# Two silu gates moved from the mixer stage into the merge, as pairs of seven products

## The chip, the cores and the metric

The kernel runs on one core of a Trainium2 chip. A core has five engines with an instruction queue each: TensorE (PE in the profile; its weight loads are PEld), VectorE (DVE), ScalarE (ACT), GpSimd (POOL) and SyncE (SP), which here only issues transfers. The metric is the device time of one execution in microseconds, lower is better.

## What is computed

One decoder layer over 1024 positions of width 1024, float32. Cut to what matters here:

```
h = rms_norm(x, norm_g) * (1 + scale) + shift          # shift, scale, gate from c @ w_ada
a_q, a_kv, a_g, a_z, b_q, b_k, b_v, b_z, c_.., d_.. = split(h @ w_in)
y_a = nsa_attention(...)             # compressed, selected and window parts
y_b = banded_attention(..., sink)    # window of 128
y_c = stick_breaking_attention(...)
y_d = retention(...)
for i, (y, z) in enumerate(((y_a, a_z), (y_b, b_z), (y_c, c_z), (y_d, d_z))):
    yi = y * silu(z)                              # 1024 x 256
    term = sigmoid(h @ w_merge[i]) * (yi @ w_br[i])
    merged = term if merged is None else merged + term
out = rms_norm(x + gate * (merged @ w_out), final_g)
```

The change is about `a_z` to `d_z`, above all the gates `silu(z)` of branches D and B.

## The kernel before

**Number format.** Every operand of a large matmul is split into a rounded high part and the rest (`hh` and `hl` for `h`, `whi` and `wlo` for weights, `yh` and `yl` for a branch's result, `phi` and `plo` for `w_br`). A product is three matmuls: high by high, rest by high, high by rest. The high part is a copy on ScalarE, the rest a subtraction on VectorE or GpSimd that follows it.

**Stages.** (1) A prologue loads x and `w_ada` and makes `h` (`hh`, `hl`), stored transposed: 8 blocks of 128 channels by 1024 positions. (2) The mix computes the four attention branches. It consists of groups, named by branch and pair of heads (`C0a`, `C0b`, `D0`, `C1`, `D1`, `A0`, `A1`, `B0`, `B1`), each of some units (front and back), and of items. An item is a projection of `h` onto 128 columns of `w_in`: 8 blocks x 3 matmuls x 2 halves of 512 positions = 48 matmuls of 128x512, a weight load of 512 KB and its split. Items with no dependence on the groups fill TensorE between the groups' short matmuls. (3) The merge takes the branches in the order C, D, A, B and computes `h @ w_merge[i]`, mostly as a Strassen-like scheme: a pair of two 128-channel tiles by two 512-position halves takes 7 products of 12 matmuls (`product`) in place of 8. The stationary sides come from the pair's two weight tiles (`op(n)`), the moving sides are seven fixed arrays `MOVING = [b11, T2, T1, b21, T3, b22, b12]`, four of them quarters of `h`, three sums of these. For 4 tiles (`PLAIN`) the product is plain. Behind each product `term` multiplies `yi @ w_br[i]` (6 matmuls on `yh`, `yl`) with the gate. (4) The w_out block loads w_out (`wr`), makes sums of its quarters (`w_jobs`), and computes the last tiles of the merge beside it. (5) The output block does merged @ w_out in 4 pairs of 7 products, adds x and applies the last norm; 124 us from the end of the merge's pairs to the last matmul.

**Order.** Within a stage the program notes its operations with their dependences first, and a list scheduler (`Program.schedule`, line 320 on) then writes an order for each engine, by a priority: a rank by dependence plus a number from two tables, `SHIFT_PE` and `SHIFT`, keyed by the label of the operation. Each engine runs its operations strictly in the order written. `noted(tc, late)` opens such a block; with `late` over zero the scheduler takes all engines but TensorE and SyncE as taken for the first `late` ns, since they are still at work from the block before. Three blocks are opened so: the merge with 8000, the w_out block and the output block with 0.

**Names.** All noted instructions carry line 380 (`issue`, which calls them) in the profile, so they are told apart by tiles. `s`, `d`, `t`, `y` are PSUM tiles of the pools; `y<-hi,RV` are the attention's last products. In the order rows further down, a tile has its buffer's number behind it.

**The gate items.** `z_item` (line 690) is an item whose result z goes to ScalarE (`tanh` of z/2), VectorE ((tanh + 1) * z) and GpSimd (times y), half by half; for branches A, B and D the product is then written to DRAM (`yd`) from GpSimd's queue. D's and C's items (`it_zcd`) stand after A's query items, A's between B's, and B's (`it_zb`) are held until groups `B0` and `B1`. In the merge `y_load` and `y_part` read `yd` back and split it into `yh` and `yl`; for the first branch, C, the split is made from SBUF ahead of the merge (line 403 in the profile).

**The sums.** `t_unit(k)`, k = 0 to 3 (label `sums`), makes `T2`, `T1`, `T3` and the last quarter's difference from `hh` and `hl`: 12 VectorE operations, 4 copies on ScalarE, 1 subtraction on GpSimd and 8 writes to DRAM (`td`) for each k. It stands after the item `it_zcd[1]`.

**Start of the last blocks.** The w_out block begins with the four loads of `wr`. `w_jobs` then splits the first quarter (`tt<-wr` on ScalarE, the subtraction on VectorE), and one of its steps is taken with each step of the plain tiles. The output block begins with the split of the fourth sum of w_out (`wt<-wst`, four on ScalarE and four on VectorE; label `wt4`) and the loads of the gate and of the final norm's scale (`gateb`, `fgb`).

Of the kernel before, what the change touches and what calls it, by code (L numbers as in the profile page):

```python
# [88 lines left out]
def chunks(w):  # L89
# [21 lines left out]
    ('first', 2): 700, ('first', 3): 10000, ('first', 5): -9990, ('first', 6): 10100,  # L111
# [3 lines left out]
    ('item', 10): -97, ('item', 11): 10033, ('item', 12): 9910, ('item', 17): 9997,  # L115
    ('item', 18): 10000, ('item', 19): 21000, ('item', 2): -9903, ('item', 20): 0,
# [77 lines left out]
class Program:  # L194
# [128 lines left out]
    def schedule(self):  # L323
# [11 lines left out]
        for i in range(len(ops)):  # L335
            if left[i] == 0:
                heapq.heappush(later[ops[i].eng], (0.0, i))
        order = []
        dma = warm = 0.0
        port = {"pool": 0.0, "dve": 0.0}  # L340
        turned = False
        while len(order) < len(ops):
# [1718 lines left out]
```

## Time and profile before

| | us |
|---|---|
| median of 3 runs | 1078.72 (1078.55 to 1079.52) |
| the profiled execution | 1079.71 |
| its span | 1077.9 |
| TensorE busy in the span | 1040.4 |
| VectorE busy | 796.5 |
| ScalarE busy | 584.4 |
| GpSimd busy | 435.5 |

The mean granted clock of TensorE over the profiled execution is 0.988 of full speed. The profile is read by stage, since the shares differ by stage: the mix from 21.5 to 587.2 us, the merge from there to 944.2 us, and the last two blocks to 1068.5 us. In the timeline the start of a matmul is recorded and its end modelled, so the distance of two starts tells more than a duration.

### The profile page before, as it was taken

How to read it: one execution, taken by the hardware profiler on the slowest of the kernel's cores; microseconds unless marked ns; L12 is line 12 of the kernel's file. 1: busy time of each engine (PE TensorE's matmuls, PEld its weight loads, DVE VectorE, ACT ScalarE, POOL GpSimd, SP SyncE). 2: the span in 40 equal slices, each digit the busy share in tenths (PEclk: the TensorE clock that was granted, in tenths of full speed). 3: DMA queues.
4: the chain of work that ended last, by engine and by line, in shares of the span. 5: the costliest groups of instructions: out<-in, count | busy, mean ns of one | idle time of the engine just before them, and what ended most of it. 6: DMA issues, size and time to landing. Idle time of an engine off the chain costs nothing.

```text
span 1077.9 us, 16022 instructions
## 1 busy us (share of the span) xinstructions
PE 1040.4 (97%) x5391; PEld 873.4 (81%) x5391; DVE 796.5 (74%) x1797; ACT 584.4 (54%) x1281; POOL 435.5 (40%) x483
## 2 busy tenths in 40 slices
PE   5999999999999999999999999999999999998996
PEld 4778888889878898888888788888888888876885
DVE  5559976986558877999875346777785565489897
ACT  5699964994348866767874232333333233346343
POOL 4623214213525466655464122255454555430002
PEclk8999999999999999999999999999999999999998
DMA  9763311102321113314313913322322232262232
GB/s 338 259 201 80 83 25 48 33 21 59 54 79 40 30 40 101 107 62 134 103 55 124 350 53 88 98 69 69 88 88 58 54 90 73 73 230 74 77 107 95
DMA packets 117606, 105.47 MB, mean 98 GB/s; under 512 B 15260, under 2 KB 96212, under 8 KB 116756
## 3 DMA queue, kind: packets, MB, share of 16 engines
q1 hardware_dynamic: 116048, 99.95, 30.3%
q0 software_dynamic: 1408, 4.48, 1.3%
q8 instruction: 42, 0.69, 0.3%
q14 instruction: 40, 0.33, 0.1%
q10 hardware_dynamic: 68, 0.02, 0.0%
HBM read 81.88 MB, written 17.83 MB: 93 GB/s over the span
## 4 chain that ended last, share of the span: by engine, by line
PE 70%; DVE 11%; ACT 6%; issue 5%; DMA 5%; POOL 2%; SPq 1%; POOLq 0%; ACTq 0%; DVEq 0%
PE d L380 25%; PE s L380 22%; PE t L380 14%; PE y L380 8%; DVE SP L380 4%; ACT t L380 2%; DVE lo L380 1%; DMA wst<-in_w_merge_dram 1%; DVE t L380 1%; ACT SP L380 1%; ACT whi L380 1%; DVE FA L380 1%; POOL RA L380 1%; DMA RA<-RA 1%; ACT hi L380 1%
## 5 line engine op out<-in xcount | busy, mean ns | idle before, releaser
L380 POOL TENSOR_TENSOR wlo<-wst,whi 128x512 fp32r<-128x512 f32 (+1 forms) x108 | 143.3, 1337 | 214.4 <-ACT whi L380 208.8
L380 PE MATMUL d<-hh,whi 128*128 128x512 f32 x440 | 180.5, 410 | 2.5 <-ACT hh L380 1.8
L380 ACT ACTIVATE whi<-wst 128x512 fp32r<-128x512 f32 (+2 forms) x121 | 89.0, 739 | 164.7 <-PE s L380 47.3
L380 PE MATMUL d<-hh,wlo 128*128 128x512 f32 x440 | 173.4, 394 | 0.0
L380 PE MATMUL d<-hl,whi 128*128 128x512 f32 x440 | 173.0, 394 | 0.0
L380 PEld LDWEIGHTS d<-hh,wlo 128*128 128x128 f32 x440 | 83.4, 190 | 18.7
L380 PEld LDWEIGHTS d<-hh,whi 128*128 128x128 f32 x440 | 83.6, 190 | 15.3 <-ACT hh L380 2.0
L380 DVE TENSOR_TENSOR lo<-t,hi 128x512 fp32r<-128x512 f32 (+2 forms) x132 | 79.8, 624 | 18.2 <-ACT hi L380 17.4
L380 PEld LDWEIGHTS d<-hl,whi 128*128 128x128 f32 x440 | 83.5, 190 | 11.6 <-DVE hl L380 0.4
L380 ACT ACTIVATE hi<-t 128x512 fp32r<-128x512 f32 (+3 forms) x148 | 73.8, 525 | 31.4 <-PE t L380 26.9
L380 POOL TENSOR_TENSOR acc<-acc,mt 128x512 f32<-128x512 f32 x44 | 68.0, 1547 | 44.3 <-DVE mt L380 43.7
L380 PE MATMUL s<-hh,whi 128*128 128x512 f32 x200 | 80.4, 402 | 3.9 <-ACT whi L380 3.9
L380 PE MATMUL s<-hh,wlo 128*128 128x512 f32 x200 | 79.7, 398 | 0.9 <-DVE wlo L380 0.9
L380 PE MATMUL s<-hl,whi 128*128 128x512 f32 x200 | 78.5, 394 | 0.0
L380 PE MATMUL t<-kbt,SP 128*128 128x128 f32 (+1 forms) x470 | 68.3, 274 | 6.8 <-DMA kbt<-in_kb_dram 6.4
L380 POOL TENSOR_SCALAR SP<-SP,den,gates 128x640 f32<-128x640 f32 (+7 forms) x64 | 52.9, 835 | 52.9 <-DVE den L380 20.7
L380 ACT ACTIVATE SP<-SP,mx 128x257 f32<-128x257 f32 (+9 forms) x96 | 62.3, 651 | 11.9 <-DVE mx L380 10.7
L380 DVE TENSOR_TENSOR mt<-s,mt 128x512 f32<-128x512 f32 x61 | 41.2, 686 | 36.4 <-PE s L380 36.1
L380 PEld LDWEIGHTS t<-kbt,SP 128*128 128x128 f32 (+1 forms) x470 | 54.7, 141 | 14.2 <-DMA kbt<-in_kb_dram 6.4
L380 PE MATMUL s<-tt,whi 128*128 128x512 f32 x192 | 59.1, 389 | 0.0
L380 ACT ACTIVATE mt<-mt 128x512 f32<-128x512 f32 x56 | 35.1, 629 | 35.4 <-DVE mt L380 35.2
L380 ACT ACTIVATE t<-t 128x512 f32<-128x512 f32 (+5 forms) x97 | 50.1, 522 | 1.1
(343 smaller groups left out, 2717.7 us busy)
## 6 DMA issues: line engine op xcount, KB each, us to landing
wst<-in_w_merge_dram SPq DMA_DIRECT2D x32, 512.0 KB, 4.8
wst<-in_w_in_dram SPq DMA_DIRECT2D x26, 512.0 KB, 3.9
td<-FA SPq DMA_DIRECT2D x32, 256.0 KB, 2.4
tt<-td SPq DMA_DIRECT2D x6, 1024.0 KB, 10.2
FA<-in_x_dram SPq DMA_DIRECT2D x8, 512.0 KB, 5.5
pst<-in_w_br_dram SPq DMA_DIRECT2D x32, 128.0 KB, 2.2
ga<-in_w_ada_dram SPq DMA_DIRECT2D x16, 256.0 KB, 3.1
wr<-in_w_out_dram SPq DMA_DIRECT2D x4, 1024.0 KB, 9.1
```

Source lines behind the costliest of these rows:

```text
L380: fn(*args, **kw)
```

## The change

1. `z_item` is no longer used for D and B. Their weights are loaded as items of the merge (`it_z`), two in front of D's and two in front of B's. The list of pairs gets an entry `(i, -1)` in front of branches 1 (D) and 3 (B): the two 128-column tiles of z by two halves as 7 products. The four quarters that come out are gated by the new `y_part`: tanh on ScalarE, two operations on VectorE, then the split into `yh` and `yl`; `y_load` reads the ungated y back, a quarter at a time, into a buffer shared with `term`. Branch A keeps the old way (renamed `y2_load`, `y2_part`).
2. y of D and B is written to DRAM ungated by SyncE at the end of each of their groups.
3. `t_unit` and the write of `hd` come after group `D1`, where they came after `it_zcd[1]`.
4. `op(7q + 6)` comes one step earlier in a pair.
5. The w_out block is opened with `late` 2000, the output block with 6000; in such a block the scheduler also takes the first transfer as later by `late` + 1100 ns, and TensorE as warm from the start.
6. The `wt4` splits and the loads of `gateb` and `fgb` move from the head of the output block to its second product.
7. Both tables are new throughout; `SHIFT` now has entries for the merge's pairs (`out` and `op` with numbers from 0 on).

```diff
 SHIFT_PE = {
-    ('A0', 0): -9000, ('A0', 1): 19710, ('A0', 11): -10020, ('A0', 14): -10000, ('A0', 15): -10300,
+    ('A0', 1): 1000, ('A0', 10): -9800, ('A0', 11): -10020, ('A0', 12): 9700, ('A0', 13): 0,
...
-        dma = warm = 0.0
+
+        dma, warm = (self.late + 1100.0, 3400.0) if self.late else (0.0, 0.0)
...
-    it_zcd = [z_item(c0 + P * p, br, p) for br, c0 in (("D", D_Z), ("C", C_Z)) for p in range(2)]
+    it_zc, it_za = [[z_item(c0 + P * p, br, p) for p in range(2)] for br, c0 in (("C", C_Z), ("A", A_Z))]
...
-    it_za = [z_item(A_Z + P * p, "A", p) for p in range(2)]
-    it_zb = [z_item(B_Z + P * p, "B", p) for p in range(2)]
...
-    it_zb[0].after = "B0"
-    it_zb[1].after = "B1"
...
+    it_z = []
+    for c0 in (D_Z, B_Z):
+        for p in range(2):
+            it = add_item()
+            mtile_weights(it, [win(c0 + P * p)])
+            it_z.append(it)
     n_mix = len(order)
-    order = order + it_m
+    for i in range(4):
+        order = order + it_z[i - 1:i + 1] * (i % 2) + it_m[8 * i:8 * i + 8]
...
+            if name[0] in "DB":
+                sy.dma_start(yd["DAB".index(name[0]), int(name[1])], Y[name[0], int(name[1])])
             md.bulk = True
+            if name == "D1":
+                for v in range(2):
+                    sy.dma_start(hd[v], b12[v].bitcast(F32))
+                for k in range(4):
+                    md.label = "sums", k
+                    t_unit(k)
...
-            if it is it_zcd[1]:
-                for v in range(2):
-                    sy.dma_start(hd[v], b12[v].bitcast(F32))
-                for k in range(4):
-                    md.label = "sums", k
-                    t_unit(k)
...
-        pairs = [(i, j) for i in range(4) for j in range(4) if (i, 2 * j) not in PLAIN]
+
+        pairs = [(i, j) for i in range(4) for j in range(-(i % 2), 4) if (i, 2 * j) not in PLAIN]
+        real = [q for q, (i, j) in enumerate(pairs) if j >= 0]
...
+        def y_load(q, e, n):
+            sy.dma_start(keep[5 - q % 2], yd[pairs[q][0] - 1, e][:, n * 512:n * 512 + 512])
...
+        def y_part(q, e, n, z, s):
+
+            y = keep[5 - q % 2]
+            se.activation(s, z, AF.Tanh, scale=0.5)
+            ve.scalar_tensor_tensor(z, s, 1.0, z, op0=ALU.add, op1=ALU.mult)
+            ve.tensor_tensor(z, z, y, ALU.mult)
+            ypart(z, e, n)
...
+            if z:
+                y_part(q, 0, 1, t1, ga)
+                y_load(q, 1, 0)
+                y_part(q, 1, 0, u3, u2)
+                return
...
-        with md.noted(tc):
+        with md.noted(tc, 2000.0):
...
-        with md.noted(tc):
-            md.label = "wt4", 0
-            for k in range(4):
-                parts(wt4, k, t4f[k], ve)
-            sy.dma_start(gateb, gd.partition_broadcast(P))
-            sy.dma_start(fgb, final_g.partition_broadcast(P))
+        with md.noted(tc, 6000.0):
...
+                if q == 0:
+                    md.label = "wt4", 0
+                    for k in range(4):
+                        parts(wt4, k, t4f[k], ve)
+                    sy.dma_start(gateb, gd.partition_broadcast(P))
+                    sy.dma_start(fgb, final_g.partition_broadcast(P))
```

How the order written out moves, at three places. A row is one instruction (or some alike) with what it writes and reads.

VectorE at the end of group D1 and the start of A0, before: `yt<-y,mv,rs` is D's last norm, the `RW`, `RA` and `vcr` rows are preparation of branch A.

```order
L380 TENSOR_SCALAR yt_150<-y_137,mv_166,rs_167 128x64
L380 TENSOR_TENSOR t_129<-t_129 32x128
L380 TENSOR_SCALAR yt_150<-y_137,mv_166,rs_167 128x64
L380 COPY sg_168<-t_127 128x32
L380 SCALAR_TENSOR_TENSOR RW<-d_133,kbt,RW 64x512
L380 TENSOR_TENSOR RA<-s_136,RA 64x32 x2
L380 TENSOR_TENSOR vcr<-s_134,vcr 32x64
L380 SCALAR_TENSOR_TENSOR RW<-d_133,kbt,RW 64x512
L380 TENSOR_TENSOR vcr<-s_134,vcr 32x64
L380 TENSOR_TENSOR RA<-d_132,RA 64x512 x2
```
The same place after the change; the `FA` rows are the sums of `t_unit`:

```order
L438 TENSOR_SCALAR yt_150<-y_137,mv_166,rs_167 128x64 x2
L438 TENSOR_TENSOR RW<-t_131,RW 128x512
L438 TENSOR_TENSOR RA<-SP,RA 64x4x64 x4
L438 TENSOR_TENSOR FA<-FA 128x512
L438 TENSOR_TENSOR FA<-FA,hh 128x512
L438 TENSOR_TENSOR FA<-FA,hl 128x512
L438 TENSOR_TENSOR FA<-hh,FA 128x512
L438 SCALAR_TENSOR_TENSOR RW<-d_132,kbt,RW 64x512 x2
L438 TENSOR_TENSOR t_129<-t_129,s_135 32x256
L438 TENSOR_TENSOR FA<-FA 128x512
L438 TENSOR_TENSOR t_129<-t_129 32x128
```
The sums now begin beside the preparation of A; before, the first of them came behind A0's units.

TensorE at the end of the mix, before: `y<-hi,RV` are branch B's last attention products, `d<-hh,whi` and `s<-hh,whi` are bulk matmuls, and 24 of the `s` rows follow before the first `d<-yh,phi`, a matmul on the split result of branch C.

```order
L380 MATMUL y_137<-hi_143,RV 128x256
L380 MATMUL y_137<-lo_149,RV 128x256
L380 MATMUL d_133<-hh,whi_138 128x512
L380 MATMUL d_133<-hl,whi_138 128x512
L380 MATMUL d_133<-hh,wlo_139 128x512
L380 MATMUL d_133<-hh,whi_138 128x512
L380 MATMUL d_133<-hl,whi_138 128x512
L380 MATMUL d_133<-hh,wlo_139 128x512
L380 MATMUL s_134<-hh,whi_141 128x512
L380 MATMUL s_134<-hl,whi_141 128x512
```
After:

```order
L438 MATMUL y_137<-hi_143,RV 128x256
L438 MATMUL y_137<-lo_149,RV 128x256
L438 MATMUL s_134<-hh,wlo_142 128x512
L438 MATMUL s_134<-hh,whi_141 128x512
L438 MATMUL s_134<-hl,whi_141 128x512
L438 MATMUL s_134<-hh,wlo_142 128x512
L438 MATMUL d_133<-yh,phi_5542 128x512
L438 MATMUL d_133<-yl,phi_5542 128x512
L438 MATMUL d_133<-yh,plo_5543 128x512
```
Four bulk matmuls now stand between the last attention product and the first one that reads `yh`.

ScalarE at the head of the output block, before: `whi<-acc` and `whi<-s` are high parts of stationary sides for the products, `wt<-wst` the four copies of the fourth sum of w_out.

```order
L380 ACTIVATE mt_5803<-t_127 128x512
L380 ACTIVATE whi_141<-acc 128x512
L380 ACTIVATE hh<-wr_8148 128x512
L380 ACTIVATE whi_141<-acc 128x512
L380 ACTIVATE wt_8475<-wst_125 128x512 x2
L380 ACTIVATE wt_8475<-wst_126 128x512 x2
L380 ACTIVATE whi_138<-s_5801 128x512
L380 ACTIVATE mt_5802<-t_140 128x512
```
After:

```order
L438 ACTIVATE whi_141<-acc 128x512
L438 ACTIVATE whi_138<-acc 128x512
L438 ACTIVATE hh<-wr_8164 128x512
L438 ACTIVATE mt_5566<-s_134 128x512
L438 ACTIVATE whi_141<-s_5565 128x512
L438 ACTIVATE wt_8487<-wst_125 128x512 x2
L438 ACTIVATE wt_8487<-wst_126 128x512 x2
```
The four `wt<-wst` now stand behind `whi<-s`.

## Rows read from the trace of the kernel before

**Rows 1.** The page: its first part, and one queue group of its sixth.
```profile
PE 1040.4 (97%) x5391; PEld 873.4 (81%) x5391; DVE 796.5 (74%) x1797; ACT 584.4 (54%) x1281; POOL 435.5 (40%) x483
...
wst<-in_w_merge_dram SPq DMA_DIRECT2D x32, 512.0 KB, 4.8
```

**Rows 2.** Busy time by stretch: us, each engine's busy (instructions), clock, DMA share, GB/s.
```profile
587.20:944.20 357.00, 356.78 (x1580) 294.98 (x1579) 224.58 (x331) 118.51 (x210) 158.08 (x127) 1.00 0.33 99
944.20:1068.50 124.30, 119.49 (x514) 97.39 (x512) 113.97 (x180) 52.72 (x102) 16.70 (x14) 0.96 0.32 115
302.30:408.10 105.80, 103.53 (x614) 88.63 (x614) 79.40 (x316) 72.69 (x195) 51.39 (x71) 1.00 0.16 43
408.10:511.50 103.40, 103.23 (x614) 89.21 (x613) 94.20 (x293) 70.75 (x177) 60.72 (x68) 1.00 0.33 105
511.50:581.40 69.90, 69.77 (x394) 58.59 (x393) 50.42 (x180) 48.31 (x135) 37.52 (x66) 1.00 0.28 86
438.50:495.10 56.60, 56.43 (x339) 48.70 (x338) 54.88 (x168) 41.16 (x97) 32.70 (x34) 1.00 0.27 89
...
995.00:1000.00 5.00, 5.00 (x13) 3.90 (x14) 0.39 (x1) 0.00 (x0) 0.00 (x0) 0.52 0.97 388
```

**Rows 3.** The chain of waits, one piece in the merge: start, us, what.
```profile
624.84 2.72 PE t L380 x12
```

**Rows 4.** Timeline of 943 to 954 us: start, us, engine, operation, idle before.
```profile
944.19 1.67 ACT L380 ACTIVATE tt<-wr 128x512 fp32r<-128x512 f32 x3 [5.50 <-DMA wr<-in_w_out_dram]
...
945.34 0.39 PE L380 MATMUL d<-hh,wlo 128*128 128x512 f32 x1
...
946.60 0.50 PE L380 MATMUL s<-hh,whi 128*128 128x512 f32 x1 [0.88 <-ACT whi L380]
...
952.22 0.40 PE L380 MATMUL d<-yl,phi 128*128 128x512 f32 x1
```

**Rows 5.** Timeline of 988 to 1001 us, the output block's first products.
```profile
989.87 0.39 PE L380 MATMUL d<-hh,wlo 128*128 128x512 f32 x1
...
990.48 2.19 ACT L380 ACTIVATE wt<-wst 128x512 fp32r<-128x512 f32 x4 [2.75 <-DVE hl L380]
...
992.58 0.61 ACT L380 ACTIVATE whi<-s 128x512 fp32r<-128x512 f32 x1
...
993.24 0.80 PE L380 MATMUL s<-hh,whi 128*128 128x512 f32 x1 [2.99 <-ACT whi L380]
...
1000.14 0.40 PE L380 MATMUL s<-hh,whi 128*128 128x512 f32 x1
...
1000.42 0.69 DVE L380 TENSOR_TENSOR mt<-d,mt 128x512 f32<-128x512 f32 x1 [5.03 <-PE d L380]
```

**Rows 6.** Groups by line on VectorE: busy us, mean ns of one, idle before.
```profile
L380 DVE TENSOR_TENSOR wst<-wst 128x512 f32<-128x512 f32 x14 | 22.4, 1598 | 0.5
...
L380 DVE TENSOR_TENSOR wlo<-acc,whi 128x512 fp32r<-128x512 f32 x24 | 16.2, 686 | 0.0
...
L380 DVE TENSOR_TENSOR FA<-FA 128x512 fp32r<-128x512 f32 (+1 forms) x20 | 15.6, 782 | 1.8 <-ACT FA L380 0.9 <-DMA yd<-FA 0.8
...
L380 DVE TENSOR_TENSOR FA<-FA,hl 128x512 f32<-128x512 f32 x12 | 10.0, 837 | 0.1
...
L380 DVE TENSOR_TENSOR FA<-hh,FA 128x512 f32<-128x512 f32 x8 | 6.6, 824 | 0.1
```

**Rows 7.** Timeline of 579.5 to 588 us, from the mix into the merge.
```profile
580.21 0.28 PE L380 MATMUL y<-lo,RV 128*128 128x256 f32 x1
...
580.70 0.62 ACT L403 ACTIVATE yh<-FA 128x512 fp32r<-128x512 f32 x1
...
581.36 0.69 DVE L403 SCALAR_TENSOR_TENSOR yl<-FA,yh 128x512 fp32r<-128x512 f32 x1 [0.24 <-ACT yh L403]
...
583.73 2.38 DVE L403 SCALAR_TENSOR_TENSOR yl<-FA,yh 128x512 fp32r<-128x512 f32 x2
...
587.15 0.39 PE L380 MATMUL d<-yh,phi 128*128 128x512 f32 x1
```

More of the change, by code (lines that the diff above doesn't have):

```diff
@@ L126 @@
[L126 to L131 removed]
[13 rows of a table added]
+    ('first', 0): 8970, ('first', 1): -8990, ('first', 2): 3000, ('first', 6): 3100,
[3 rows of a table added]
@@ L173 @@
-    ('split', 5): 0, ('split', 6): -100, ('sum', 0): 0, ('sum', 1): 0, ('sums', 0): 9700,
-    ('sums', 1): 10097, ('sums', 2): 2057, ('tile', 15): 19630, ('tile', 23): -1300,
[5 rows of a table removed]
[13 rows of a table added]
+    ('ada', 14): 60, ('ada', 15): 1270, ('ada', 16): -10000, ('ada', 17): 0, ('ada', 19): 0,
+    ('ada', 20): 9960, ('ada', 21): 11000, ('ada', 22): -697, ('ada', 23): -3000,
[3 rows of a table added]
+    ('item', 10): 10000, ('item', 11): 300, ('item', 13): 9987, ('item', 15): -7,
+    ('item', 16): -130, ('item', 17): -7010, ('item', 19): 20283, ('item', 2): -10300,
@@ L180 @@
+    ('out', 86): 0, ('out', 87): 9870, ('out', 89): 1000, ('out', 90): 1200, ('out', 91): 0,
+    ('out', 92): 30, ('out', 93): -10000, ('out', 95): 300, ('out', 96): 9700, ('out', 97): 100,
+    ('out', 98): 10000, ('out', 99): 11130, ('split', 0): 1897, ('split', 1): -1000,
+    ('split', 2): 100, ('split', 4): 3000, ('split', 5): 0, ('split', 6): 0, ('split', 7): 0,
+    ('sum', 0): -30, ('sum', 1): 10100, ('sums', 0): 10010, ('sums', 1): 19103, ('sums', 2): 20430,
[5 rows of a table added]
 }
@@ L1774, in pair @@
             u3 = keep[4 + q % 2]
-            first, fin = j == 0, q + 1 < len(pairs) and pairs[q + 1][1] == 0
+            z = j < 0
+            g = -1 if z else real.index(q) - 1
+            first, fin = j == 0 and i == 2, q + 1 < len(pairs) and pairs[q + 1] == (2, 0)
             o = product(7 * q + 0, MOVING[0])
-            if q:
+            if q and pairs[q - 1][1] >= 0:
                 term(q - 1, 1, 0, keep[4 + (q - 1) % 2])
+            if z:
+                y_load(q, 0, 0)
+            elif q:
                 pwprep(8 * i + 2 * j + 1)
-                if first:
-                    y_part(q, 0)
-                    y_load(q, 1)
+            if first:
+                y2_part(q, 0)
+                y2_load(q, 1)
             op(7 * q + 3)
             se.activation(t1, o, AF.Copy)
-            gate_load(q - 1, 0)
+            gate_load(g, 0)
             o = product(7 * q + 1, MOVING[1])
@@ L1790, in pair @@
             if first:
-                y_part(q, 1)
+                y2_part(q, 1)
             op(7 * q + 5)
             add(u3, o, u2)
+            op(7 * q + 6)
             yield
             o = product(7 * q + 3, MOVING[3])
-            op(7 * q + 6)
             add(g11, o, t1)
-            tanh(g11)
-            gate_sum(q - 1, 0)
-            gate_load(q - 1, 1)
+            if z:
+                y_part(q, 0, 0, g11, ga)
+                y_load(q, 1, 1)
+            else:
+                tanh(g11)
+            gate_sum(g, 0)
+            gate_load(g, 1)
             o = product(7 * q + 4, MOVING[2])
@@ L1804, in pair @@
             add(c5, o, u3)
-            term(q, 0, 0, g11)
+            if not z:
+                term(q, 0, 0, g11)
             o = product(7 * q + 5, MOVING[5])
@@ L1808, in pair @@
             add(t1, o, t1)
-            tanh(c5)
-            term(q, 1, 1, c5)
-            gate_sum(q - 1, 1)
+            if z:
+                y_part(q, 1, 1, c5, u2)
+                y_load(q, 0, 1)
+            else:
+                tanh(c5)
+                term(q, 1, 1, c5)
+            gate_sum(g, 1)
             if fin:
-                y_load(q + 1, 0)
+                y2_load(q + 1, 0)
             o = product(7 * q + 6, MOVING[6])
@@ L1819, in pair @@
             tanh(u3)
-            gate_end(q - 1)
-            i2, j2 = pairs[q + 1] if q + 1 < len(pairs) else (3, 3)
+            gate_end(g)
+            i2, j2 = next((v for v in pairs[q + 1:] if v[1] >= 0), (3, 3))
             pwprep(8 * i2 + 2 * j2)
```

110 lines of the change are left out of this document (69 added, 41 removed), and 98 rows, old and new, of tables (SHIFT, SHIFT_PE).

## Prediction

> **What bounds the kernel now.** I read the totals of the page first, then the busy time by stage, then the chain of waits, and last the timeline at the places where TensorE stops. TensorE is busy 97% of the span [rows 1], and in the middle of the kernel it never stops: 103.53 of 105.80 us, 103.23 of 103.40 and 69.77 of 69.90 in three consecutive stretches of the mix, 356.78 of 357.00 us in the merge [rows 2]. There a matmul with 512 moving columns starts every 2.72 / 12 = 0.2267 us [rows 3]. So from 302 to 944 us the time is the number of matmuls, as long as nothing else becomes the bound. Two things can. VectorE is second: 94.20 us of 103.40 in the stretch from 408.1 us, and 54.88 of 56.60 (97%) inside it, beside a TensorE that still did not lose anything (56.43) [rows 2]. And the last stage is different from the merge: from 944.20 us TensorE is busy only 119.49 of 124.30, VectorE 113.97 [rows 2].
>
> That last stage has two stops with one cause. At 944.19 us ScalarE runs three `tt<-wr`, for which it had waited 5.50 us on the DMA of w_out; the weight halves `whi<-wst` stand behind them in its queue, and TensorE, which needs them, goes from the start at 945.34 to the next one at 946.60 [rows 4]. At 990.48 four `wt<-wst`, waiting for VectorE's `hl`, stand in front of `whi<-s` (992.58); TensorE starts at 989.87 and then again at 993.24, a wait of 2.99 us [rows 5]. Behind both stops the matmuls come at half their pace: from 995 to 1000 us the granted clock is 0.52, that is the lower level of 1.2 GHz where everything before ran at 2.4, after TensorE had stood [rows 2].
>
> The sum is made against the profiled run, 1079.71 us (span 1077.9). The median is 1078.72, 1.0 us less, and the forecast is put back by that at the end.
>
> **1. Fewer matmuls.** The four gate items of D and B, 48 matmuls of 512 columns each, leave the mix: 192 x 0.2267 = -43.5 us. Two pairs of 7 products x 12 matmuls come into the merge: 168 x 0.2267 = +38.1 us. Both ends lie where TensorE is the bound, so the net is 24 x 0.2267 = **-5.4 us**, if the mix really becomes 43.5 us shorter (steps 2 and 3) and the merge only 38.1 us longer (step 4).
>
> **2. The sums move into the first half of branch A.** The 48 VectorE operations of `t_unit` ran between 408 and 522 us. In the new order 46 of them stand before unit 8 of A, that is in what was the stretch from 302.30 to 408.10 us, where VectorE was busy 79.40 us [rows 2]. Their 40 commonest take 15.6 + 10.0 + 6.6 = 32.2 us, 0.805 us each [rows 6], so 46 cost 37.0 us and VectorE gets 116.4 us there. TensorE gets more there too: counted in the two orders, 36 wide matmuls (8.2 us) and 22 narrow ones of half the columns (at half of 0.2267, 2.5 us) come into the stretch, which makes 105.8 + 10.7 = 116.5 us. Two engines with 116 us each: at the best VectorE share seen beside a full TensorE, 97%, the stretch takes 116.4 / 0.97 = 120.0 us, 3.4 more than TensorE alone; with sums that meet nothing (0.686 us, the `wlo<-acc` row [rows 6]) VectorE has 111 us and fits. I take +2.0, nearer to the dearer end since the sums' own row is the measured one. The far end is every sum at the 1.598 us of `wst<-wst` [rows 6]; that is rival 1. Behind it the stretches are easier: the next one loses about 108 matmuls (24.5 us) and some 37 us of VectorE, which leaves 79 us of TensorE beside 57 of VectorE. Step: **+2.0 (0 to 3.4)**.
>
> **3. End of the mix.** The last gate item of B filled TensorE while branch B's result was split into `yh`, `yl`. Before, the last `y` matmul starts at 580.21, the four splits run from 580.70 on ScalarE to 583.73 + 2.38 = 586.11 on VectorE, and the first matmul that reads them starts at 587.15; 30 wide matmuls (6.8 us) stand between, so nothing waits [rows 7]. In the new order 4 stand there (0.9 us). TensorE is then ready at 581.4, while the first `yl` lands at 581.36 + 0.69 = 582.05, and the later ones come about 1.1 us apart where TensorE has six matmuls (1.36 us) for each. So some 0.2 for `yh`, 0.5 for the first `yl`, 1.1 once for a split that is late, 0.3 for the rest. The least is the first `yl` alone, 0.5; the most is the whole splitting less its cover, 5.4 - 0.9, less the two groups that TensorE has by then, about 4, into which a half clock behind the stop would also have to fit. **+2.1 (0.5 to 4)**. The ungated copies of D and B that SP now writes at each group's end stand in front of later weight loads in its queue; the 512 KB loads land in 4.8 us [rows 1] and are issued an item (10.9 us) ahead, so I put them at nothing, and at 1 us if an item's load comes late.
>
> **4. The pairs in the merge.** Each gate pair adds to VectorE the sums of a normal pair and two operations per quarter more, a `tanh` on ScalarE, and four `y_load` on SP; it leaves out the two gates' terms. VectorE has 224.58 of 357.00 us there, ScalarE 118.51, GpSimd 158.08 [rows 2], so throughput does not decide. What can wait is the first term of branch D, which needs all four quarters split: 108 matmuls (24.5 us) stand between it and C's last term where there were 54. And `y_load` goes into the one of two buffers that the pair before has just left; behind it on SP wait weight loads, with the same room as above. **+0.5 (0 to 3)**.
>
> **5. The last stage.** First stop: from 945.34 to 952.22 us there are 14 starts, 14 x 0.2267 = 3.2 of 6.88 us, 3.7 lost [rows 4]. Second: from 989.87 to 1000.14, 16 starts, 3.6 of 10.27 us, 6.6 lost [rows 5]. Together 10.35 us, the half-clock stretches included. The new order puts `tt<-wr` behind the `whi` that TensorE waits for, and the four `wt<-wst` behind `whi<-s`. What is late next? Before the product that reads `whi<-s` TensorE has 228 matmuls (51.7 us) from the last product of the merge's T3, VectorE 63 operations where it had 73, some 42 us by the mean of the stretch (113.97 / 180 = 0.63 us [rows 2]) with a start 6.6 us in: 49 us against 51.7. That is near, and VectorE is at 92% over the whole stage. So I take nine tenths of the 10.35 as won: **-9.4 (-10.35 to -5)**. At the far end, where VectorE is the bound of this stage, nothing is won (rival 2).
>
> Sum: -5.4 + 2.0 + 2.1 + 0.5 - 9.4 = -10.2, so 1079.7 - 10.2 = 1069.5 for a run like the profiled one, and **1068.5** beside the median.
>
> **The rivals.** *1, slower: the sums cost more in A.* Operations of the same size and form take 0.686 us or 1.598 us in this trace [rows 6], so something doubles them in places, and branch A has GpSimd at work half of the time (51.39 of 105.80 us [rows 2]). If the sums met it each time, VectorE would have 79.4 + 46 x 1.598 = 152.9 us, at 97% a stretch of 157.6 instead of 118.6, +39: 1107.5. It turns the change to slower (over 1080.9) at 12.4 us more, that is from (131.0 x 0.97 - 79.4) / 46 = 1.04 us per sum. Against it: beside a GpSimd that was busier (60.72 of 103.40 us) they took 0.805. Chance 0.06. The Trainium skill, SBUF — State Buffer, Who interferes with whom, says that VectorE and GpSimd share one pair of ports under an exclusive lock, so that a VectorE operation with two inputs in SBUF and a GpSimd one shut each other out. By that rule the sums, which have two SBUF inputs, would be held more wherever GpSimd is busier, and it would speak against the move; the two durations of the same operation agree with such a lock, the 0.805 in the busier stretch does not make it dear.
>
> *2, the last stage is bound by VectorE.* The stops at the head go, and TensorE waits as long later for the output rows. Then step 5 is 0 and the time 1078.72 - 5.4 + 2.0 + 2.1 + 0.5 = 1077.9: no change. For it: 92% over the stage. Against: after the second stop VectorE itself idled 5.03 us for TensorE's product [rows 5], so it was not what was late. Chance 0.13.
>
> *3, the mix gets shorter by less than 43.5 us.* Without the filler of four items the chains of branches A and B show through: TensorE waits for ScalarE and VectorE between units as it does not now. At 6 us more than in steps 2 and 3 the time is 1074.5. For it: the wide matmuls between branch A's last unit and the end fall from 219 to 135. Chance 0.13.
>
> *4, the change does not do what it says at the end,* because the order written down is not what the engines meet (a DMA of w_out still late, the output rows' loads behind it), and the start is slower by a new order of the prologue: +10 to +14 on the forecast, half of it no change, half slower. Chance 0.06.
>
> **How the numbers follow.** Forecast 0.62, rivals 0.06, 0.13, 0.13, 0.06. 0.2% is 2.2 us, about what a measurement here can tell from none: faster is under 1076.6, slower over 1080.9. Faster: 0.62 + 0.13 = 0.75. Same: 0.13 + 0.03 = 0.16. Slower: 0.06 + 0.03 = 0.09. The lowest time in the bounds is -5.4 + 0 + 0.5 + 0 - 10.35 = -15.3, so 1063.4; the steps' dear ends, -5.4 + 3.4 + 4 + 3 - 5 = 0, reach 1078.7 only if all come together. The range 1063 to 1078 holds the forecast and rivals 2 and 3, about 0.85.
>
> **What the new profile would show.** Step 1: 24 matmuls fewer and a merge of about 395 us at 0.2267. Step 2: VectorE near 97% through the first half of A, the sums between 0.69 and 0.85 us, TensorE with under 3 us of waits. Step 3: a wait on `yl` of 1 to 2 us at the start of the merge. Step 5: no wait for `whi` over 0.3 us behind the merge and no slice at half clock. Wrong would be a clock dip behind the end of the mix, waits of TensorE on VectorE's `acc` or `wlo` in the output block, or sums over 1 us.

## The result and the profile after

The changed kernel takes 1086.56 us (median of 4 runs, 1084.7 to 1087.9) against 1078.63 of the kernel before in the same comparison: a ratio of 1.0073, 95% interval 1.0056 to 1.0090. It is slower by 7.9 us, where 10.1 less had been forecast. The profiled execution of it took 1087.56 us, span 1085.6.

The page of the changed kernel, its first part, answers to [rows 1]:

```profile
PE 1038.7 (96%) x5367; PEld 868.3 (80%) x5367; DVE 814.1 (75%) x1833; ACT 590.5 (54%) x1293; POOL 421.4 (39%) x467
```

24 matmuls and their 5.4 us are gone, as counted, and TensorE's share has fallen from 97 to 96%: the span grew by waiting. Where, is read by stretches with the same work at their ends. In the profiled executions:

| from, to | before, us | after, us | difference | of it matmuls | of it waiting |
|---|---|---|---|---|---|
| first matmul, branch D's first `s<-FA,SP` | 153.3 | 156.8 | +3.5 | 0 | +3.5 |
| to the end of D1 | 147.0 | 136.3 | -10.7 | -11.8 | +1.1 |
| first half of A (to its unit 8) | 109.6 | 128.9 | +19.3 | +13.2 | +6.1 |
| second half of A | 97.1 | 69.8 | -27.3 | -27.4 | +0.1 |
| branch B, to the last `y<-hi,RV` | 66.8 | 56.9 | -9.9 | -11.4 | +1.5 |
| to the first `yh` | 7.1 | 1.3 | -5.8 | -5.9 | +0.1 |
| merge and last blocks, to the last matmul | 481.0 | 519.9 | +38.9 | +37.9 | +1.0 |

(Matmuls are counted at the distance that one of its size usually has from the next, 0.2267 us with 512 columns; waiting is the rest. For narrow matmuls that distance can be taken a little differently, which moves an entry of the last two columns by up to 0.9 us.) The first row is no effect of the change: five more kernels below have the changed prologue in the same written order, and reach that place at 160.3 to 161.1 us, as the seven kernels with the old one do (159.7 to 161.4); this one execution came at 163.1. From the first matmul to the first `yh`, the four of them that keep the sums take 546.0 to 548.0 us, four kernels with the old mix 579.5 to 580.8. So the mix has become some 33 us shorter, not 43.5 less 4.1, and the last blocks, whose stops should have gone, have them still.

Busy time by stretch in the changed kernel (columns as in [rows 2]): first half of A, then the rest of the mix, the merge to its first stop, and the 38 us ahead of the second stop:

```profile
299.40:428.30 128.90, 123.83 (x724) 105.53 (x723) 116.71 (x397) 93.01 (x246) 72.41 (x83) 0.99 0.33 103
428.30:556.40 128.10, 126.59 (x781) 107.67 (x779) 102.53 (x384) 96.67 (x260) 62.46 (x104) 1.00 0.14 41
556.40:957.30 400.90, 399.60 (x1762) 328.93 (x1762) 257.48 (x383) 136.42 (x240) 165.51 (x133) 1.00 0.33 99
962.00:1000.00 38.00, 36.57 (x154) 29.12 (x153) 37.40 (x59) 19.26 (x33) 7.38 (x5) 0.97 0.19 70
```

The same two kinds of stretch in the kernel before, the first half of A and the 37 us ahead of its second stop:

```profile
306.60:416.20 109.60, 107.55 (x644) 92.42 (x645) 81.02 (x324) 76.20 (x208) 53.88 (x73) 1.00 0.18 49
953.00:990.00 37.00, 37.00 (x165) 30.52 (x163) 36.19 (x56) 19.31 (x33) 7.39 (x5) 1.00 0.20 74
```

In A's first half VectorE went from 81.02 to 116.71 us, the 36 us of the sums, and TensorE stands 5 us. The last row of each group is the one that the prediction should have asked for: ahead of the second stop VectorE was busy 36.19 of 37.00 us before and 37.40 of 38.00 after. It was full in both.

The start of the merge, timeline of the changed kernel, answers to [rows 7]:

```profile
556.37 0.69 DVE L461 SCALAR_TENSOR_TENSOR yl<-FA,yh 128x512 fp32r<-128x512 f32 x1 [0.29 <-ACT yh L461]
...
557.12 0.51 PE L438 MATMUL d<-yl,phi 128*128 128x512 f32 x1 [0.23 <-DVE yl L461]
...
557.42 1.90 DVE L461 SCALAR_TENSOR_TENSOR yl<-FA,yh 128x512 fp32r<-128x512 f32 x3
...
558.77 0.50 PE L438 MATMUL d<-yl,phi 128*128 128x512 f32 x1 [0.41 <-DVE yl L461]
```

TensorE waits twice for `yl`, 0.23 and 0.41 us by the row and 1.2 us in all.

And the two stops of the last blocks, with the transfers that SP starts ahead of the first, answers to [rows 4, 5]:

```profile
948.87 0.46 SPq L438 DMA_DIRECT2D wr<-in_w_out_dram  x1
...
949.43 0.45 SPq L438 DMA_DIRECT2D wst<-in_w_merge_dram  x1
...
956.02 0.63 ACT L438 ACTIVATE whi<-wst 128x512 fp32r<-128x512 f32 x1 [7.54 <-DMA wst<-in_w_merge_dram]
...
956.69 0.69 DVE L438 TENSOR_TENSOR wlo<-wst,whi 128x512 fp32r<-128x512 f32 x1 [5.19 <-ACT whi L438]
...
959.83 0.50 PE L438 MATMUL d<-yh,phi 128*128 128x512 f32 x1 [2.33 <-DVE mt L438]
```

```profile
999.87 1.89 DVE L438 TENSOR_TENSOR hl<-wr,hh 128x512 fp32r<-128x512 f32 x3
...
1000.61 0.50 PE L438 MATMUL s<-hl,whi 128*128 128x512 f32 x1 [1.94 <-DVE hl L438]
```

The first: SP starts 1 MB of w_out (948.87) just ahead of the merge's last weights (949.43) and three more MB right behind them (from 949.93); the weights land 6.6 us after their start, ScalarE has waited 7.54 us for them, VectorE behind it 5.19, and the `mt<-d,mt` that would free TensorE's PSUM buffer stands in VectorE's queue behind that. The second: TensorE waits for VectorE's `hl`, the last of three that VectorE, busy without a break, reaches at 999.87.

### The profile page after: what moved, and what is told of

Read it like the earlier page. It is cut to its first block, busy times and chain, and to the rows that moved or that the text cites. A ratio compares the mean times of both kernels' runs of the same rounds, so it can differ in the third digit from the quotient of the medians.

```text
span 1085.6 us, 15994 instructions
## 1 busy us (share of the span) xinstructions
PE 1038.7 (96%) x5367; PEld 868.3 (80%) x5367; DVE 814.1 (75%) x1833; ACT 590.5 (54%) x1293; POOL 421.4 (39%) x467
## 4 chain that ended last, share of the span: by engine, by line
PE 66%; DVE 15%; ACT 8%; DMA 5%; issue 3%; POOL 2%; SPq 0%; POOLq 0%; ACTq 0%; DVEq 0%
PE d L438 23%; PE s L438 21%; PE t L438 14%; PE y L438 8%; DVE SP L438 3%; DVE mt L438 2%; DMA FA<-in_w_ada_dram 2%; DVE lo L438 2%; ACT SP L438 2%; DVE FA L438 1%; ACT t L438 1%; DVE wlo L438 1%; DMA FA<-in_x_dram 1%; ACT hi L438 1%; DMA wst<-in_w_merge_dram 1%
## 5 line engine op out<-in xcount | busy, mean ns | idle before, releaser
L438 PE MATMUL d<-hh,whi 128*128 128x512 f32 x392 | 161.5, 412 | 5.1 <-DVE RW L438 2.9
L438 PE MATMUL d<-hl,whi 128*128 128x512 f32 x392 | 154.4, 394 | 2.5 <-DVE hl L438 2.5
L438 PE MATMUL d<-hh,wlo 128*128 128x512 f32 x392 | 154.6, 394 | 0.0
L438 PEld LDWEIGHTS d<-hh,wlo 128*128 128x128 f32 x392 | 74.2, 189 | 16.7
L438 PEld LDWEIGHTS d<-hh,whi 128*128 128x128 f32 x392 | 74.6, 190 | 16.3 <-DVE RW L438 3.0
L438 PEld LDWEIGHTS d<-hl,whi 128*128 128x128 f32 x392 | 74.6, 190 | 12.3 <-DVE hl L438 2.7
L438 POOL TENSOR_TENSOR acc<-acc,mt 128x512 f32<-128x512 f32 x44 | 63.8, 1457 | 43.1 <-DVE mt L438 43.0
L438 PE MATMUL t<-kbt,SP 128*128 128x128 f32 (+1 forms) x470 | 68.1, 274 | 10.2 <-DMA kbt<-in_kb_dram 6.3
L438 DVE TENSOR_TENSOR mt<-s,mt 128x512 f32<-128x512 f32 x69 | 46.5, 685 | 34.9 <-PE s L438 30.4
L438 PE MATMUL s<-tt,whi 128*128 128x512 f32 x224 | 70.3, 396 | 0.0
L438 DVE TENSOR_TENSOR wlo<-wst,whi 128x512 fp32r<-128x512 f32 x52 | 40.9, 788 | 21.6 <-ACT whi L438 21.1
```

Source lines behind the costliest of these rows:

```text
L438: fn(*args, **kw)
```

## Experiments

Several experiments need an order that stays as it is. Where an edit changes what the scheduler sees, everything behind it in the block can be written in another order; so in most of the kernels below operations are noted and scheduled as ever, and only not issued (`skip`), and the rest stands where it stood.

**The prologue's table entries as before (pro_old), and the sums left out of the program (no_sums).**

```diff
 SHIFT_PE, SHIFT: entries of mod, ada, sum, split, x, h0, h1, first
-as changed
+as before
```

> The changed kernel with the table entries of the prologue's labels (mod, ada, sum, split, x, h0, h1, first) as they were before. Reading behind it: up to the first attention product of branch D both kernels give TensorE the same work, and the changed one is 3.5 us later there, with VectorE's hl standing at 24.6 and 27.7 us where it stood at 22.4 and 23.7. If the written order of the prologue is the cause: 2.5 to 4 us less, 1082.5 to 1084. Rival, that the loads of x and w_ada simply arrived later in that execution, or that the later stages wait anyway: within 1 us of the changed kernel.

```diff
     def t_unit(k):
-        ve.tensor_tensor(d, f(b22, 0), f(b12, 0), ALU.subtract)
...
+        for i, x in enumerate((b22, b11, b12, b21)):
+            for v in range(2):
+                sy.dma_start(td[i, v, :, k], x[v][:, k].bitcast(F32))
```

> The changed kernel without the sums' arithmetic: td is filled by 32 plain copies of the quarters, so 48 VectorE, 16 ScalarE and 4 GpSimd operations are gone from the first half of branch A. If these hold up A's own chain there, the 6.2 us that this stretch lost more than before come back, all or nearly: 1080 to 1081.5. Rival, that the stretch loses its time because the gate items no longer fill TensorE (the chain of A's units is bare): at most 2 us less, 1084.5 or more, with VectorE idle instead.

Measured: 1128.2 us (1.0459, 1.0430 to 1.0488) and 1108.96 (1.0288, 1.0261 to 1.0316), 42 and 22 us slower than the changed kernel, the second with less work in it. In branch B alone TensorE waits 17 us longer in pro_old than in the changed kernel, 12 us longer in no_sums, and no_sums is 14.6 us longer in the prologue, whose code was not touched. The mix is one block for the scheduler: an edit anywhere in it gives another order everywhere, and what the order is worth is several times the terms in dispute. Neither says anything on its own question.

**The sums noted, not issued (no_sums2).**

```diff
+            op.skip = eng != "sp" and self.label is not None and self.label[0] == "sums"
...
-            for fn, args, kw in self.ops[i].calls:
+            for fn, args, kw in [] if self.ops[i].skip else self.ops[i].calls:
```

> The changed kernel in exactly its written order, but the sums' operations on VectorE (48), ScalarE (16) and GpSimd (4) are noted and then not issued, so the four sums hold other data. In the run without sums the whole mix had been written in another order; here only the operations are gone. If the sums hold up branch A's chain in its first half: the 21.7 us that TensorE loses from the end of D1 to unit 8 (15.5 before) fall to 16 or less, the time to 1080 to 1082. Rival, that this stretch is long because fewer bulk matmuls cover A's chain: 20 us or more remain lost there, 1085 or more.

Measured: 1083.42 us (1.0052, 1.0037 to 1.0067), 3.1 less than the changed kernel, of which the prologue may be a part. The first half of A takes 126.5 us instead of 128.9, with VectorE at 87.72:

```profile
297.10:423.60 126.50, 123.11 (x726) 106.16 (x725) 87.72 (x351) 84.47 (x231) 58.37 (x80) 0.97 0.34 105
```

So without the sums the stretch is 2.4 us shorter, beside the 2.0 (0 to 3.4) of step 2, and neither expectation fits: 3.7 of the 6.1 us are something else. In both kernels TensorE stands at the same instruction. Timelines, the changed kernel and then this one:

```profile
318.53 0.29 PE L438 MATMUL s<-w2t,sg 64*32 64x64 f32 x2
...
320.12 1.51 DVE L438 SCALAR_TENSOR_TENSOR RW<-d,kbt,RW 64x512 fp32r<-64x512 f32 x2 [0.71 <-ACT RW L438]
...
321.69 0.50 PE L438 MATMUL d<-hh,whi 128*128 128x512 f32 x1 [2.87 <-DVE RW L438]
```

```profile
317.79 1.51 DVE L439 SCALAR_TENSOR_TENSOR RW<-d,kbt,RW 64x512 fp32r<-64x512 f32 x2 [0.71 <-ACT RW L439]
...
319.36 0.80 PE L439 MATMUL d<-hh,whi 128*128 128x512 f32 x1 [2.88 <-DVE RW L439]
```

2.87 and 2.88 us for `RW<-d,kbt,RW`, VectorE's last step in emptying the PSUM buffer of a projection of A, which alternates between ScalarE and VectorE. The four other kernels below with this order have the same stop, 2.87 or 2.88 us. Behind it the granted clock falls to its lower level, 1.2 GHz, for 3.4 us in the changed kernel, whose first half of A is otherwise at 2.4 GHz, as all of it is in the kernel before:

```profile
322.60:326.00 3.40, 3.40 (x12) 2.82 (x11) 3.25 (x15) 2.11 (x9) 2.27 (x2) 0.50 0.20 63
```

The nine matmuls that start there take 1.8 us at their usual distance, so the stop and the clock behind it make some 4.5 us. Without the sums the low clock lasted longer, 6.8 us (318.3 to 325.1), so the 2.4 us understate what the sums cost: dep_skip, a run below with this order, the sums and 6.9 us of low clock, takes 129.9 us for the first half of A, and beside it the sums cost 3.5 us. The changed order has 36 more bulk matmuls up to the end of A's first unit, pulled forward where the gate items no longer fill. That these are why the buffer is late was not tried by itself.

**Gate items of D and B not issued in the old order (no_z); those of C (no_zc); those and the sums (no_zc_sums).**

```diff
     def half(it, evac, n):
         ps = pools["d"].tile([P, 512], F32, name=f"d{it.idx}_{n}", tag="d")
+        md.drop = it in it_zcd[:2] + it_zb
         yield from mm3(ps, it.hi, it.lo, n * 512)
         evac(ps, n)
+        md.drop = False
```

> The kernel before in exactly its written order, with the gate items of D and B noted and then not issued: 192 matmuls, 8 operations on ScalarE, 8 on VectorE and 8 on GpSimd gone, the weight loads and splits left in, y of D and B not gated. The prediction counted 192 x 0.2267 = 43.5 us for them, since TensorE was never idle in the mix: 1035 for that. In the changed kernel the mix got 30.8 us shorter up to the first yh. If the gate items were also the cover of the attention chains, part of the 43.5 us turns into waits of TensorE, here too where the order is the old one and the sums stand at their old place: 1041 to 1048.

Measured: 1075.47 us, 0.9976 (0.9966 to 0.9987). 192 matmuls, 43.5 us of TensorE, are gone and the time falls by 3.1. Two stretches from which they are gone, in no_z and, below, in the kernel before:

```profile
342.90:416.40 73.50, 61.88 (x365) 50.94 (x364) 55.41 (x212) 49.05 (x128) 34.35 (x46) 0.93 0.14 44
514.40:582.40 68.00, 57.75 (x307) 48.29 (x306) 46.10 (x172) 45.61 (x126) 35.85 (x63) 0.85 0.27 85
```

```profile
342.50:416.20 73.70, 72.78 (x462) 64.31 (x461) 58.12 (x216) 52.11 (x133) 39.23 (x50) 1.00 0.14 44
513.30:580.10 66.80, 66.67 (x375) 55.80 (x374) 48.32 (x175) 46.19 (x128) 36.92 (x64) 1.00 0.28 85
```

A's units take 73.50 us where they took 73.70, branch B 68.00 where it took 66.80; TensorE's busy time fell by 10.9 and 8.9, and its granted clock from 1.00 to 0.93 and 0.85. Most of the gate items had been laid into time in which the attention chain kept TensorE waiting anyway. Part of it is the clock: it was at its lower level for 10.2 us of the first stretch and for 20.5 us of the second, where it fell within a stop of 3.17 us for VectorE's `FA` (matmul starts 554.64 and 558.10):

```profile
557.10:577.60 20.50, 12.52 (x43) 10.21 (x44) 7.74 (x21) 9.31 (x22) 11.77 (x15) 0.50 0.24 75
```

The matmuls that start in these pieces would take 4.8 and 5.9 us at their usual distance, so at most that much of the two stretches is owed to the clock, against some 12 and 10 us in which TensorE's rows show it waiting. An estimate from these numbers: at the full clock at most 3.1 + 4.8 + 5.9 = 13.8 of the 43.5 us would have come back. What did come back by itself are the 5.8 us behind the last `y<-hi,RV`, where nothing else ran.

```diff
+        md.drop = it in it_zcd[2:]
```

> The kernel before in its written order with the two gate items of C noted and not issued: 96 matmuls (21.8 us), which stand between A's units 7 and 12, where VectorE was busy 94 of 103 us and the sums run. The four items of D and B, 43.5 us, had given back 3.1. If TensorE is the bound in this stretch: 1057. If VectorE with the sums takes over at its 97%: at most 5 us less, 1073.5. If A's units wait for each other here as they did beside D's items: 1077 or more.

```diff
+            op.skip = (self.drop or self.label is not None and self.label[0] == "sums") and ...
```

> no_zc with the sums' operations (48 on VectorE, 16 on ScalarE, 4 on GpSimd) also not issued. The changed kernel has this stretch 27 us shorter with 27 us of matmuls fewer and the sums gone from it. If the sums (VectorE) are what held it long in no_zc: 15 us or more less than no_zc, down to 1057. If the chain of A's units holds it: within 3 us of no_zc.

Measured: 1077.93 us, 0.9994 (0.9985 to 1.0004), that is nothing for 21.8 us of matmuls; and 1070.97, 0.9929 (0.9915 to 0.9944), 7.0 less than no_zc. The stretch with most of C's items, between the ends of A's units 7 and 12, before, in no_zc, and in no_zc_sums:

```profile
409.46:460.00 50.54, 50.54 (x296) 43.47 (x294) 45.24 (x155) 35.67 (x95) 30.73 (x36) 1.00 0.34 110
```

```profile
409.92:459.27 49.35, 38.80 (x209) 32.05 (x207) 42.28 (x151) 33.95 (x92) 25.60 (x33) 0.83 0.34 113
```

```profile
409.59:454.24 44.65, 36.45 (x208) 30.46 (x206) 30.54 (x131) 30.60 (x85) 21.55 (x32) 0.92 0.49 154
```

The stretch takes 50.54, 49.35 and 44.65 us, with VectorE busy 45.24, 42.28 and 30.54. With its filler gone it is held by the units' chain, in which VectorE, at 86%, is the busiest engine, and in part by the clock, which in no_zc is at its lower level for 17.1 us (416.3 to 433.4, matmuls worth 5.3 us at their usual distance). With the sums gone too, 4.7 us of it give, and the low clock lasts 6.8 us; how much of the 4.7 is the clock was not tried. Neither of my two ends held: 7 us, not 3 and not 15.

**The last two blocks as before, on the changed kernel (tail_old), and the changed ones on the kernel before (before_tail).**

```diff
-        with md.noted(tc, 2000.0):
+        with md.noted(tc):
...
-        with md.noted(tc, 6000.0):
+        with md.noted(tc):
+            (wt4 splits, gateb, fgb)
 and the tables' entries of these blocks as before
```

> The changed kernel with the last two blocks as before: late 0 for both, the wt4 splits and the two loads back at the head of the output block, and the table entries of these blocks as before (numbers shifted by 14). The prediction's step 5 would have this dearer by 9.4 us: 1096. Reading of the trace: the last blocks lost 10.35 us before and about 8.7 now, since each stop has been replaced by another: 1.7 us dearer, 1088. Rival: the old blocks behind the new merge meet the same weight load and VectorE, no difference, 1086.

> The kernel before with the changed last two blocks alone: late 2000 and 6000, the wt4 splits and two loads at the second product, and the changed tables' entries for these blocks (numbers shifted by -14). Step 5 of the prediction gave it -9.4: 1069. The run tail_old, the reverse on the changed kernel, cost 7.0. If the gain stands by itself: 1069 to 1072. If the new entries only fit the changed merge: 1077 or more.

Measured: tail_old 1093.58 us (1.0136, 1.0119 to 1.0153), 7.0 dearer than the changed kernel; before_tail 1077.13 us, 0.9988 (0.9978 to 0.9997), 1.4 us faster than the kernel before and the fastest here of those that leave nothing out. Lost in the last blocks (by the starts of 512-column matmuls, as in step 5): 10.4 us before, 7.8 in before_tail; 14.3 in tail_old, 8.7 in the changed kernel. So the new blocks are worth 2.6 us by themselves and 5.6 behind the new merge, which by itself makes the old ones dearer by 3.9. In before_tail TensorE still stops, at other instructions, for VectorE's `mt` and `wlo`:

```profile
965.08 0.50 PE L379 MATMUL d<-yh,phi 128*128 128x512 f32 x1 [1.93 <-DVE mt L379]
...
988.32 0.50 PE L379 MATMUL s<-hh,wlo 128*128 128x512 f32 x1 [1.71 <-DVE wlo L379]
```

In tail_old there are two stops again, larger than before, and the first is now behind the weights' transfer, as in the changed kernel:

```profile
956.43 0.63 ACT L440 ACTIVATE whi<-wst 128x512 fp32r<-128x512 f32 x1 [7.82 <-DMA wst<-in_w_merge_dram]
...
961.20 0.50 PE L440 MATMUL d<-yh,phi 128*128 128x512 f32 x1 [3.57 <-DVE mt L440]
```

```profile
1004.85 2.19 ACT L440 ACTIVATE wt<-wst 128x512 fp32r<-128x512 f32 x4 [3.43 <-DVE hl L440]
...
1007.61 0.80 PE L440 MATMUL t<-hh,whi 128*128 128x512 f32 x1 [4.45 <-ACT whi L440]
```

**w_out's loads held back behind the last weights, on the changed kernel (wr_dep) and on the kernel before (before_dep).**

```diff
+            w = st.q[-2].t[:, 0:1]
+            for t in (r11, r12, r22, r21):
+                po.tensor_tensor(t[:, 0, 0:1], w, w, ALU.subtract)
             for t, kh, n in ((r11, 0, 0), (r12, 0, 1), (r22, 1, 1), (r21, 1, 0)):
                 sy.dma_start(t, wo_v[:, 4 * kh:4 * kh + 4, 512 * n:512 * n + 512])
```

> The changed kernel with the four loads of w_out held back until the last weight load has landed (four one-column GpSimd operations that read its tile write into theirs). If the first stop (TensorE at 959.83, 2.33 us, then half clock) comes from that weight load sharing the DMA engines with the first load of w_out, ScalarE's wait of 7.54 us shrinks to about 4.5 and the stop goes: 3 to 4 us less, 1083, unless w_out's later arrival makes the second stop longer by as much (rival, 1086). If the weight load is late for another reason (its buffer): 1086 to 1088.

> The kernel before with w_out's four loads noted behind the last weight loads and held back until these have landed, as in wr_dep. If the first stop of the kernel before was also these weights sharing the DMA engines with w_out (rather than ScalarE's order, as the prediction had it), its 3.7 us go: 1075 to 1076, unless w_out's later arrival adds to the second stop. Rival, ScalarE's order alone: no change or slower, 1078 to 1081.

Measured: wr_dep 1082.69 us (1.0039, 1.0024 to 1.0054), 3.9 less than the changed kernel, some of it possibly the prologue's 3 us in the profiled run; the loss in the last blocks fell from 8.7 to 4.9 us, the first stop from 4.2 to 1.4. Its timeline:

```profile
947.48 0.37 SPq L438 DMA_DIRECT2D wst<-in_w_merge_dram  x1
...
951.70 0.63 ACT L438 ACTIVATE whi<-wst 128x512 fp32r<-128x512 f32 x1 [5.13 <-DMA wst<-in_w_merge_dram]
...
951.97 2.20 SPq L438 DMA_DIRECT2D wr<-in_w_out_dram  x4
...
957.09 2.20 ACT L438 ACTIVATE tt<-wr 128x512 fp32r<-128x512 f32 x4 [2.17 <-DMA wr<-in_w_out_dram]
```

The weights, started at 947.48, land within 4.2 us, ScalarE has them at 951.70 instead of 956.02, and w_out, issued 3 us later, is ready at 957.09. So the first stop of the changed kernel was the two transfers side by side. On the kernel before the like edit, with the four loads also noted behind the last weight loads, costs 5.0 us (1083.53; 1.0047, 1.0030 to 1.0064):

```profile
949.16 2.19 ACT L380 ACTIVATE tt<-wr 128x512 fp32r<-128x512 f32 x4 [5.00 <-DMA wr<-in_w_out_dram]
...
951.77 0.50 PE L380 MATMUL d<-yh,phi 128*128 128x512 f32 x1 [3.87 <-DVE mt L380]
```

There ScalarE now waits 5.00 us for w_out, with VectorE's `mt` behind it, and TensorE stops 3.87 us: its first stop was not that of the changed kernel, and holding w_out back is no cure for it: the theory that both kernels have one first stop falls. The prediction's reading of it, ScalarE's order behind the transfer of w_out, fits these rows too, but no run tried it by itself.

**Half of the last splits' subtractions on GpSimd (dep_pool) or not issued (dep_skip, before_skip).**

```diff
-                    parts(d, k, src[:, k], e)
+                    parts(d, k, src[:, k], po if k % 2 else ve)
```

> The changed kernel with w_out's loads held back as in wr_dep, and with every second one of the last 12 subtractions of w_out's splits on GpSimd, where VectorE had all. In wr_dep VectorE was busy 27.00 of 27.00 us ahead of the second stop, GpSimd 5.81. If VectorE's load is the cause of the second stop, six operations less (4.1 us) make it shorter by 2 to 4 us: 1079 to 1081. Rival, that GpSimd and VectorE then hold each other up: VectorE's operations beside it take up to 1.6 us and nothing is won or some is lost, 1082.5 to 1085.

```diff
+                    md.drop = k % 2 == 1          # op.skip = self.drop and eng == "dve"
                     parts(d, k, src[:, k], e)
+                    md.drop = False
```

> The kernel before in its written order, with 6 of the last 12 subtractions of w_out's splits (VectorE, 0.69 us each, 4.1 in all) noted and then not issued; ScalarE's wt copies still stand in front of whi. If the second stop (TensorE from 989.87 to 993.24, 6.6 us with the half clock) is VectorE's amount of work, the hl for which the wt copies waited is there 4 us sooner and the stop is gone or nearly: 1072 to 1074.5. If it is the order on ScalarE, as the prediction had it, the four copies still hold up whi for 2.2 us and some 3 us or more stay: 1075.5 or more.

> wr_dep (1082.7) with the same 6 subtractions noted and not issued, in its order. If VectorE's amount of work makes the stops at 992 to 996 us (3.5 us with all): 1079 to 1080. If they come from where the new order puts single operations: 1081.5 to 1083. Where six more GpSimd operations had been put in place of these six (dep_pool) the time was 1087.4.

Measured: dep_pool 1087.39 us (1.0086, 1.0070 to 1.0101), 4.7 dearer than wr_dep. The timeline shows why:

```profile
985.68 6.15 POOL L438 TENSOR_TENSOR hl<-wr,hh 128x512 fp32r<-128x512 f32 x3 [12.18 <-ACT hh L438]
...
991.79 3.40 POOL L438 TENSOR_TENSOR yl<-wr,yh 128x512 fp32r<-128x512 f32 x2
...
993.99 4.03 DVE L438 TENSOR_TENSOR wlo<-acc,whi 128x512 fp32r<-128x512 f32 x3
995.15 1.72 POOL L438 TENSOR_TENSOR hl<-wr,hh 128x512 fp32r<-128x512 f32 x1
...
995.79 0.80 PE L438 MATMUL s<-hh,wlo 128*128 128x512 f32 x1 [2.76 <-DVE wlo L438]
```

GpSimd's six subtractions follow each other from 985.68 to 996.87, the first in 2.76 us, the others in 1.71 to 1.75 each. VectorE's three `wlo` meet the last two of them:

```profile
L438 DVE TENSOR_TENSOR wlo<-acc,whi x3: 678/1745/1762, 994.0 to 997.3; 128x512 fp32r<-128x512 f32 x3
```

(Shortest, median and longest in ns.) Two beside GpSimd took 1.75 and 1.76 us, the third, behind it, 0.68, the usual time. What VectorE was relieved of it lost again, and TensorE stopped 2.76 us for `wlo`.

before_skip: 1075.80 us, 0.9975 (0.9963 to 0.9987), 2.8 less than before; the second stop's loss fell from 6.7 to 4.1 us, and what is left stands behind the `wt` copies:

```profile
987.38 2.19 ACT L382 ACTIVATE wt<-wst 128x512 fp32r<-128x512 f32 x4 [1.33 <-DVE hl L382]
...
990.14 0.50 PE L382 MATMUL s<-hh,whi 128*128 128x512 f32 x1 [1.58 <-ACT whi L382]
```

dep_skip: 1081.62 us (1.0025, 1.0015 to 1.0034), 1.1 less than wr_dep; the loss there fell from 3.4 to 2.0. So 4.1 us of VectorE's work taken away gave 2.6 of 6.7 us in the one and 1.4 of 3.4 in the other. VectorE's amount and the order on ScalarE both hold the second stop; neither theory alone fits. The shares are rough, each from one execution: in before_skip the first stop, ahead of every operation left out, lost 1.8 us where it had lost 3.7.

## Why the prediction was wrong

**Step 1** counted right and concluded wrong. The matmuls are 24 fewer, 5.4 us, and the merge's 168 cost what they should. But "where TensorE is the bound" was read from its busy share, 103.53 of 105.80 us [rows 2], and no_z shows that there it was not: without the 43.5 us the time fell by 3.1, and by at most 13.8 with the lower clock taken off. A share of 98% in a stretch with movable filler can mean that the filler covered the waits, and not that it was the limit. The 30.8 us (some 33 without that execution's prologue) by which the changed mix did get shorter had to come from another order altogether: 27 us of matmuls and the sums left A's second half together, 13 us of matmuls went into the first. Rival 3 named the mechanism, at a chance of 0.13 and 6 us. no_z shows it in the old order; that it made the waits of the changed mix, no run shows. With the waits for `yl` the mix came 9.8 us short of steps 1 to 3 in the profiled execution, about 7 without the prologue.

**Step 2** was about right for the sums: +2.0 forecast, 2.4 measured, 3.5 at a like clock. The 40 that took 0.805 us each before took 0.76, and VectorE's 116.4 us came out as 116.71. TensorE's share was too low: 10.7 us more were counted, 13.2 came, since 34 narrow matmuls of half the columns and not 22 entered between the marks of the table. And the stretch lost 6.1 us: the rest goes with the projection whose PSUM buffer is late, a stop of 2.87 us and 3.4 us of half clock behind it, for which the step has no term. Rival 1, which would have made the sums dear, did not happen: GpSimd was busy 72.41 of 128.90 us beside them, yet only four of the 46 took over 1.04 us, where the rival turns the change to slower if all do. The mechanism behind it showed up in dep_pool, 1.75 us beside GpSimd against 0.68. The Trainium skill, SBUF — State Buffer, Who interferes with whom, has a VectorE instruction with two inputs in SBUF and a GpSimd one that reads SBUF exclude each other on a shared pair of ports; these two durations agree.

**Step 3** was right: 1.2 us for `yl` (+2.1, 0.5 to 4), and no half clock behind it.

**Step 4** was near: the merge to its first stop took 42.5 us more, 40.1 of it matmuls (177 starts), 1.2 step 3, so 1.2 us against 0.5 (0 to 3).

**Step 5** is the largest miss: 1.7 us won of 9.4. The two rows on which it rested are the ends of two chains, and I took the instruction in front, on ScalarE, for the cause. In the row of the second stop stood what it waited for, VectorE's `hl` [rows 5], and VectorE was busy 98% of the 37 us before it. I divided VectorE's work by the mean over the whole last stage, 49 us against 51.7, called that near, and took nine tenths. Rival 2 named this at 0.13. It also overlooked what the new merge does to the blocks behind it: tail_old shows 3.9 us more in the same blocks, 1.8 of it at the first stop, behind a weight load beside w_out's. What made the second dearer no run separates: VectorE was no fuller ahead of it, 39.25 of 42.00 us (964 to 1006). Against that, the new blocks won 5.6 us. "Later" stops took the place of those removed, which the text asked about and answered too kindly.

Between the forecast for an execution like the profiled one, 1069.5, and its 1087.56 lie 18 us: 9.8 in the mix with the waits for `yl` (2 to 3 of them that execution's prologue), 7.7 in the last blocks and 0.7 in the pairs.

What stays open is why the PSUM buffer in A's first half is late, what the 1.5 us in B are, and how much another order of the same work could win: pro_old and no_sums show 20 to 40 us between orders, both times for the worse.

## What to carry to other kernels

A stretch where the first engine is 98% busy with work that was placed to fill its waits need not be bound by that engine: issue the same order without the filler, and see what the stretch then takes, before pricing the filler at its own duration. Read the granted clock of that run too: where TensorE stood without its filler, the clock fell, and part of the length is that. Ahead of a stop, look at each engine's share of the 30 or 40 us before it and not only at the instruction that came last; where an engine is at 98% there, leave out some of its work and see how much of the stop goes, before taking the instruction in front for the whole cause. And where a scheduler writes the order, undo a part by leaving instructions out of a fixed order, since any edit that the scheduler sees moves everything.

## What was not expected of the hardware

Two transfers side by side: 512 KB of weights landed in 4.2 us alone (947.48 to 951.70 in wr_dep) and in 6.6 when 1 MB had been started 0.6 us ahead of them and three more behind (949.43 to 956.02). Subtractions of 128x512 on VectorE took 1.75 us beside GpSimd's of 1.72, and 0.68 when GpSimd was done (dep_pool). One execution's prologue came 2 to 3 us later than that of five other kernels in the same order.
